# Two-layer hybrid decoder step, one core: four head groups' mixers rearranged (one delta-net pass, four-page attention, fillers in the gated mixer, weight loads on another queue)

## Chip, cores and metric

One Trainium2 chip, one of its cores. The metric is the device time of one execution in microseconds (us), lower is better. A profiled execution also gives a span, from the first to the last instruction of the program. The engines: PE is TensorE (PEld its weight loads), DVE is VectorE, ACT is ScalarE, POOL is GpSimd, SP is SyncE, which here only issues DMAs. [...]

## The reference

544 tokens (a prompt of 512 and 8 samples of 4) pass two layers; everything is f32. In each layer one input projection (1024 to 3592 columns) feeds four head groups that are 256 wide:

```python
u = x @ p['w_in'][l]
(a_in, a_gb, a_gc, b_qkv, b_a, b_b, b_z,
 c_q, c_f, c_i, c_g, d_q, d_k, d_v) = _split(u, SPLITS)
y_a = a_gb * causal_dwconv(a_gc * a_in)                  # A: gated short conv
y_b = rms_norm(gated_delta(q, k, v, beta, g)) * silu(b_z)  # B: gated delta net
y_c = rms_norm(gla(silu(c_q), k_c, c_i, log_f)) * silu(c_g) # C: HGRN2 (gated linear attention)
y_d = rms_norm(diff_attention(d_q, d_k, d_v))            # D: differential attention
x = layer_norm(ALPHA * x + concat(y_a, y_b, y_c, y_d) @ w_o)
x = layer_norm(ALPHA * x + ffn(x))   # layer 0: SwiGLU; layer 1: top-2-of-8 SwiGLU experts
```

B and C are chunked scans that also carry a state; per chunk B solves a unit-triangular system. D attends, for the prompt, within the 512 tokens; for each sample over 16 cached pages of 128 rows, named by a page table, and its own 4 new rows. The outputs are y, the new K and V rows, and the conv and scan states.

## The kernel before, in words

**Order.** The code is written against a tile framework, which lays down each engine's instruction order at build time: a statement earlier in the program has precedence, a later one is pulled into places where the earlier ones are not ready by the framework's own timing model. [...] A tile pool with `bufs=n` hands out n buffers in turn; a new tile waits until the buffer's last user is done.

**Projections.** All large matmuls run at f32r in three passes (high times high, high times low, low times high). `split_w` (L352) loads a 128-column weight tile of 512 KB into `wraw` (three buffers), SP issuing the DMA (L364); ACT (L368), in the expert layer DVE too (L366), makes the high part `wh` and DVE the low part `wl`. `dense` (L380) then issues 48 matmuls for a tile: 8 k-blocks, three passes, two token halves of 256 and 288 columns (in the trace "st", for its PSUM tiles; all matmuls go through the helper `mm`, L290). `win` (L497) does one tile of `w_in`; there are 29 per layer.

**Mixers** (`mixers`, L477, once per layer). PSUM has eight banks: three for projections (`stp`), three `dx` for D, two `mx` for B and C. In program order, at its end (L1261 to L1287):

- `d_in` (L569): 6 tiles for q, k, v of D; K and V go out by POOL's queue.
- `mix_b` (L712): 7 tiles with the conv, gates and norms. Then `g_half` (L811) twice, each for two of the four heads and all four chunks. It builds the 128x128 systems, gathers their 16x16 diagonal blocks through DRAM (`sd`, `bk`), solves them by 15 steps of product and sum on DVE over 64 partitions (L888 is the sum), writes them back through DRAM (`te`), doubles the inverse to 32, 64 and 128 by small matmuls, and runs the four-chunk recurrence. A sample part follows. The second half shares the first half's buffers (`GB = 1`).
- `d_attn` (L588): `d_sample` (L596) has two groups of four samples, and in each 16 steps of one page a sample. A step loads four pages of 256 KB (K and V together, SP's queue, nine buffers that the heads share, L616), takes scores with 8 matmuls (`qs` as weights, 32 columns, each sample in its own column group, 128 keys as moving data), row maximum (L632), exponential with sum (L634), one transpose (L635), a copy on DVE (L637), 4 value matmuls, and on DVE a masked product `r` and its sum (L603) into `pj`. After every second step comes one of 16 prompt `d_head`s (L676), with two score matmuls of 32 rows, one after the other, each into a `dx` bank, and a third bank for the transposed weights. `rms_d` (L536) norms D's and B's output.
- `dc.close()` (L1278), then `hook`, which loads the residual for the next norm into the memory that is freed.
- `mix_a` (L1231): 6 tiles. Then `mix_c` (L1072): 8 tiles; per token half-width `i` seven decay levels over 512 tokens (POOL subtracts, ACT exponentiates, DVE multiplies, `level`, L1106), four chunks of some 45 small matmuls (64x32, 64x64, 32x32), a sample part. Then 2 tiles of `b_z`.
- The four outputs are split into high and low parts and go to `out_proj` (L1445).

Of the kernel before, what the change touches and what calls it, by code (L numbers as in the profile page):

```python
# [10 lines left out]
F32 = mybir.dt.float32  # L11
# [4 lines left out]
OP = mybir.AluOpType  # L16
# [23 lines left out]
KVB = 9  # L40
# [5 lines left out]
ARR = 6  # L46
# [140 lines left out]
def _pack(a):  # L187
# [19 lines left out]
    f["kv"] = _cols(np.concatenate([kp, a["cache_v"].reshape(L, npool, 128, 256)], 3))  # L207
# [58 lines left out]
def _body(ctx, tc, I, O):  # L266
# [15 lines left out]
    stp = pool(ctx, "stp", 3, PSUM)  # L282
# [66 lines left out]
    wq = [S] * WQ0  # L349
    wpools, wcount = [wp], [0]  # L350

    def split_w(parts, n):  # L352
# [10 lines left out]
        for a, src in enumerate(parts):  # L363
            (wq.pop(0) if wq else SP).dma_start(r if na == 1 else r[:, a], src)  # L364
# [112 lines left out]
    def mixers(l, y32, hook):  # L477
# [5 lines left out]
        xps = pool(mc, "mx%d" % l, 2, PSUM)  # L483
# [13 lines left out]
        def win(n, i):  # L497
            w = first.pop(0) if first else load_w(I["w_in"][l, WT0[n] + i])
            res = halves(stp, "st")
            dense(res, w, xh, xl, KT)  # L500
            return res
# [67 lines left out]
        def d_in():  # L569
            q = win_arr("d_q", 32.0 ** -0.5, y32[:, 6:8])  # L570
            k = win_arr("d_k")
            G.dma_start(O["k"][l].rearrange("a p t -> p a t"), k)
            v = win_arr("d_v")
# [14 lines left out]
        def d_attn(q, k, vt, qs):  # L588
            heads = [d_head(q, k, vt, qb, tl, h2) for qb in range(4) for tl in range(2) for h2 in range(2)]
            for n, _ in enumerate(d_sample(k, vt, qs)):  # L590
                if n % 2 == 1:
                    heads[n // 2]()
            for i in range(2):
                rms_d(y32[:, 6:8], i, nd[:, l:l + 1])

        def d_sample(k, vt, qs):  # L596
            od = y32[:, 6:8]
            ends = []

            def select(pj, po):  # L600
# [4 lines left out]
            regs = []  # L605

            def page(i):
                if i == len(regs):
                    with ExitStack() as qx:
                        if len(ends) > 8:  # L610
                            qx.enter_context(tc.issue_after(ends[-9].ins))
                        _, r = nc.values_load_multi_w_load_instructions(ptb[:, i:i + 8], engines=[mybir.EngineType.SP],
                                                                        min_val=0, max_val=I["kv"].shape[1] - 1)
                    regs.extend(r)
                t = dq.tile([128, 512], F32, name="kv", bufs=KVB)
                ends.append(SP.dma_start(t, I["kv"][l][bass.ds(regs[i], 1)].rearrange("o p f -> p (o f)")))  # L616
                return t

            for g in range(2):
                nm = dq.tile([128, 20], F32, name="nm", bufs=2)  # L620
                zz = dq.tile([128, 20], F32, name="zz", bufs=2)
                pj = dq.tile([128, 17, 64], F32, name="pj", bufs=1)
                for j in range(16):
                    kv = [page(64 * g + 4 * j + b) for b in range(4)]
                    ps = dx()
                    for tl in range(2):
                        for b in range(4):
                            mm(ps[32 * b:32 * b + 32, 0:128], qs[:, tl, 4 * g + b, :], kv[b][:, 128 * tl:128 * tl + 128],
                               start=tl == 0, stop=tl == 1)
                    if j == 15:  # L630
                        tt(V, ps[:, 0:128], ps[:, 0:128], bs[:, 0:128], OP.add)
                    V.reduce_max(nm[:, j:j + 1], ps[:, 0:128], axis=AX.X, negate=True)  # L632
                    e = dq.tile([128, 128], F32, name="e", bufs=3)
                    S.activation(e, ps[:, 0:128], AF.Exp, bias=nm[:, j:j + 1], accum_out=zz[:, j:j + 1])  # L634
                    PE.transpose(ps[:, 128:256], e, ident)  # L635
                    et = dq.tile([128, 128], F32, name="et", bufs=3)
                    V.tensor_copy(et, ps[:, 128:256])  # L637
                    for b in range(4):
                        mm(ps[32 * b:32 * b + 32, 256:512], et[:, 32 * b:32 * b + 32], kv[b][:, 256:512])
                    select(pj[:, j], ps[:, 256:512])  # L640
                    yield
# [5 lines left out]
                V.reduce_max(nm[:, 16:17], ps[:, 0:32], axis=AX.X, negate=True)  # L647
                sn = dq.tile([128, 32], F32, name="sn", bufs=1)
                S.activation(sn, ps[:, 0:32], AF.Exp, bias=nm[:, 16:17], accum_out=zz[:, 16:17])
                pe = dx()  # L650
                PE.transpose(pe[0:32, 0:128], sn, ident)
                etn = dq.tile([32, 128], F32, name="etn", bufs=1)
                V.tensor_copy(etn, pe[0:32, 0:128])
                po = dx()
                for b in range(4):
                    mm(po[32 * b:32 * b + 32, 0:256], etn[:, 32 * b:32 * b + 32], vt[0:32, 4, :])
                select(pj[:, 16], po[:, 0:256])
                V.tensor_reduce(nm[:, 17:18], nm[:, 0:17], axis=AX.X, op=OP.min)
                wj = dq.tile([128, 17], F32, name="wj", bufs=1)
                S.activation(wj, nm[:, 0:17], AF.Exp, bias=nm[:, 17:18], scale=-1.0)  # L660
                tt(V, zz[:, 0:17], zz[:, 0:17], wj, OP.mult)
# [1430 lines left out]
```

## Time and profile before

| | us |
|---|---|
| median of 3 runs (2251.12 to 2275.32) | 2256.49 |
| the profiled execution | 2249.46 |
| its span | 2247.8 |
| mixers of layer 0, from the last projection of `mix_b` to the first full out-projection | 108 to 487 |
| mixers of layer 1, the like | 1075 to 1434 |

The profiled execution's 2249.46 us is its span and 1.7 us around it. The page counts as busy what an engine's instructions cover; a matmul's end is modelled, so that TensorE's busy share says little of its pace. Its pace is read from the count of matmuls in a stretch (x) and from the distance between starts.

### The profile page before, as it was taken

What the parts mean: (1) busy time and instruction counts of PE and PEld (TensorE: products, weight loads), DVE (VectorE), ACT (ScalarE), POOL (GpSimd) and SP (SyncE); (2) the same over time, 40 slices, a digit from 0 to 9 for tenths busy, and PEclk for the clock granted to TensorE, in tenths of its full rate; (3) what the DMA queues carried; (4) which work ended last, traced back from release to release, by engine and by line L of the source; (5) the groups of instructions that cost most, each with busy time, mean ns of one, the idle gap of its engine ahead of it and who ended that gap; (6) DMA issues with size and microseconds to landing.
All of it is one profiled execution on the core that took longest, in us unless ns stands there. A gap on an engine that the chain in (4) does not pass through costs nothing.

```text
span 2247.8 us, 47097 instructions
## 1 busy us (share of the span) xinstructions
PE 2094.8 (93%) x18052; PEld 1846.0 (82%) x18052; DVE 1495.4 (67%) x2944; ACT 821.1 (37%) x1842; POOL 460.7 (20%) x588
## 2 busy tenths in 40 slices
PE   8999999998999999999999999888999998898896
PEld 7977776778999999989777667777899897797885
DVE  4676755767333334645767666679989987777795
ACT  3522424455231223444324344434333433433221
POOL 0101012112000000111110221003514436535431
PEclk9999997989999999999999999889999899999998
DMA  6344343233322323542444343337778686586751
GB/s 236 99 125 145 112 144 111 87 118 102 95 79 84 100 86 90 173 160 87 150 126 131 116 131 97 119 113 247 252 235 272 205 278 200 174 264 202 270 190 61
DMA packets 147314, 340.92 MB, mean 152 GB/s; under 512 B 24099, under 2 KB 34568, under 8 KB 147080
## 3 DMA queue, kind: packets, MB, share of 16 engines
q1 hardware_dynamic: 131944, 317.02, 44.0%
q0 software_dynamic: 6032, 18.67, 2.5%
q10 hardware_dynamic: 9104, 2.13, 0.5%
q8 instruction: 144, 2.36, 0.4%
q14 instruction: 90, 0.74, 0.1%
HBM read 319.91 MB, written 17.85 MB: 150 GB/s over the span
## 4 chain that ended last, share of the span: by engine, by line
PE 68%; DVE 12%; POOL 7%; issue 5%; ACT 4%; DMA 4%; DVEq 0%; SPq 0%; ACTq 0%; POOLq 0%
PE st L290 34%; PE ff L290 12%; PE mx L290 9%; PE dx L290 8%; DVE wl L293 3%; POOL m_g L293 2%; PE ee L290 2%; POOL m_u L293 2%; DVE wh L366 2%; ACT wh L368 1%; POOL hg L293 1%; POOL r L1402 1%; ACT ev L1668 1%; DMA sd<-d 1%; DMA wraw<-in_m_g_dram 1%
## 5 line engine op out<-in xcount | busy, mean ns | idle before, releaser
L293 DVE TENSOR_TENSOR wl<-wraw,wh 128x1024 fp32r<-128x1024 f32 (+2 forms) x474 | 562.0, 1194 | 284.8 <-ACT wh L368 261.4
L290 PE MATMUL st<-xh,wh 128*128 128x256 f32 (+1 forms) x1536 | 465.4, 304 | 15.0 <-ACT wh L368 11.6
L290 PE MATMUL st<-xl,wh 128*128 128x256 f32 (+1 forms) x1536 | 462.0, 301 | 8.4 <-DVE xl L293 8.4
L290 PE MATMUL st<-xh,wl 128*128 128x256 f32 (+1 forms) x1536 | 461.4, 301 | 1.8 <-DVE wl L293 1.8
L368 ACT ACTIVATE wh<-wraw 128x1024 fp32r<-128x1024 f32 (+2 forms) x280 | 274.0, 980 | 480.6 <-PE st L290 281.8
L290 PEld LDWEIGHTS st<-xh,wh 128*128 128x128 f32 x1536 | 297.6, 194 | 32.8 <-ACT wh L368 12.7
L290 PEld LDWEIGHTS st<-xl,wh 128*128 128x128 f32 x1536 | 297.8, 194 | 25.7 <-issue 13.4
L290 PEld LDWEIGHTS st<-xh,wl 128*128 128x128 f32 x1536 | 297.3, 194 | 22.0 <-issue 17.7
L290 PE MATMUL st<-xg,wh 128*128 128x416 f32 (+4 forms) x880 | 253.7, 363 | 28.1 <-ACT ev L1668 26.1
L290 PE MATMUL st<-xg,wl 128*128 128x208 f32 (+4 forms) x880 | 217.9, 248 | 4.1 <-DVE wl L293 3.7
L290 PEld LDWEIGHTS st<-xg,wh 128*128 128x128 f32 x880 | 171.1, 194 | 35.8 <-ACT ev L1668 33.1
L290 PEld LDWEIGHTS st<-xg,wl 128*128 128x128 f32 x880 | 173.7, 197 | 9.1 <-DVE wl L293 9.0
L366 DVE CAST wh<-wraw 128x1024 fp32r<-128x1024 f32 (+2 forms) x194 | 158.9, 819 | 21.3 <-PE ee L290 12.0
L290 PE MATMUL st<-hg,wh 128*128 128x416 f32 (+4 forms) x440 | 126.8, 366 | 2.5 <-POOL hg L293 2.2
L1402 POOL TENSOR_SCALAR r<-r,par 128x256 f32<-128x256 f32 (+1 forms) x32 | 29.2, 924 | 467.6 <-ACT xh L1401 467.5
L290 PE MATMUL st<-hg,wl 128*128 128x208 f32 (+4 forms) x440 | 110.2, 251 | 2.1 <-DVE wl L293 2.1
L290 PE MATMUL ff<-hh,wl 128*128 128x256 f32 (+1 forms) x352 | 103.2, 293 | 3.3 <-DVE wl L293 3.2
L290 PE MATMUL st<-wh,xg 128*128 128x256 f32 x528 | 104.7, 292 | 0.0
L290 PE MATMUL ff<-hh,wh 128*128 128x256 f32 (+1 forms) x352 | 103.0, 293 | 0.4 <-ACT wh L368 0.4
L290 PE MATMUL ff<-hl,wh 128*128 128x256 f32 (+1 forms) x352 | 102.1, 290 | 0.0
L290 PE MATMUL ff<-xh,wl 128*128 128x256 f32 (+1 forms) x352 | 101.8, 289 | 0.0
L290 PE MATMUL ff<-xl,wh 128*128 128x256 f32 (+1 forms) x352 | 101.6, 289 | 0.0
(580 smaller groups left out, 4324.5 us busy)
## 6 DMA issues: line engine op xcount, KB each, us to landing
kv<-in_kv_dram SPq DMA_DIRECT2D x256, 256.0 KB, 3.8
wraw<-in_w_in_dram SPq DMA_DIRECT2D x57, 512.0 KB, 3.7
wraw<-in_m_g_dram SPq DMA_DIRECT2D x54, 512.0 KB, 4.3
wraw<-in_m_u_dram SPq DMA_DIRECT2D x54, 512.0 KB, 4.3
wraw<-in_m_g_dram SPq DMA_DIRECT2D x65, 256.0 KB, 4.2
wraw<-in_m_u_dram SPq DMA_DIRECT2D x65, 256.0 KB, 4.6
wraw<-in_w_o_dram SPq DMA_DIRECT2D x32, 512.0 KB, 3.5
wraw<-in_m_d_dram SPq DMA_DIRECT2D x40, 384.0 KB, 3.6
```

The costliest lines, as they stand in the source:

```text
L290: return PE.matmul(out, lhsT, rhs, start=start, stop=stop)
L293: return e.tensor_tensor(out, a, b, op=op)
L366: V.tensor_copy(h, r)
L368: S.activation(h, r, AF.Copy)
L1402: G.tensor_scalar(ri[:, u], ri[:, u], gcol[:, u:u + 1], bcol[:, u:u + 1], op0=OP.mult, op1=OP.add)
L1668: S.activation(t[:, 0:2 * cap], ps[:, 0:2 * cap], AF.Copy)
```

## The change

What it does, part by part:

- **B**: `mix_b` becomes `b_in` (projections), `b_chunks` and `b_sample`. `b_chunks` does all four heads in one pass: 16 systems at once, one gather through DRAM, one substitution over 128 partitions, one recurrence with both token halves in a chunk step. The output overwrites v.
- **D**: K and V pages are two tensors; a step takes four pages of four samples. Scores of 512 keys fill one bank, in 16 matmuls of 256 moving columns (two pages each), now with the sample as the outer loop and the two 128-row parts inside; one maximum, one exponential, four transposes, one copy on ACT, 16 value matmuls that add up in PSUM, one masked product and sum. Seven buffers hold two pages of K or V each. A group has 4 steps, not 16. A head's two score matmuls are issued together, its transposed weights reuse a score bank, and one scaling moves from DVE to ACT. Heads are spread over 20 yields.
- **Order**: `d_in`, `b_in`, `b_chunks`, `c_in` (six tiles of C), `d_attn`, `hook`; then `b_sample` and `mix_c`, whose levels are made per 256 tokens, with four yields. At each yield two fillers run: `mix_a`'s two rows, its stores, z 0, z 1, g 0, g 1 (z with B's norm and gate).
- **Weights**: within the mixers POOL's queue issues the weight loads, not SP's.
- **PSUM**: `dx` 3, `mx` 3, projections 2 within the mixers; the three-bank pool opens behind them.

```diff
-KVB = 9
+KVB = 5
+PGB = 7
-ARR = 6
+ARR = 5
...
-            (wq.pop(0) if wq else SP).dma_start(r if na == 1 else r[:, a], src)
+            (wq.pop(0) if wq else wdef[0]).dma_start(r if na == 1 else r[:, a], src)
...
-        xps = pool(mc, "mx%d" % l, 2, PSUM)
+        xps = pool(mc, "mx%d" % l, 3, PSUM)
+        stm = pool(mc, "st%d" % l, 2, PSUM)
...
             for n, _ in enumerate(d_sample(k, vt, qs)):
-                if n % 2 == 1:
-                    heads[n // 2]()
+                while done < 16 and done < (n + 1) * 16 / 20:
+                    heads[done]()
+                    done += 1
...
-                for j in range(16):
-                    kv = [page(64 * g + 4 * j + b) for b in range(4)]
+                for j in range(4):
+                    regs = indices(64 * g + 16 * j)
                     ps = dx()
-                    for tl in range(2):
-                        for b in range(4):
-                            mm(ps[32 * b:32 * b + 32, 0:128], qs[:, tl, 4 * g + b, :], kv[b][:, 128 * tl:128 * tl + 128],
-                               start=tl == 0, stop=tl == 1)
+                    for u in range(2):
+                        for b, t in enumerate(pages("kc", regs, u)):
+                            for tl in range(2):
+                                mm(ps[32 * b:32 * b + 32, 256 * u:256 * u + 256], qs[:, tl, 4 * g + b, :],
+                                   t[:, :, 128 * tl:128 * tl + 128], start=tl == 0, stop=tl == 1)
...
+                    e = soft(ps, j, 512)
+                    yield
+                    for a in range(4):
+                        PE.transpose(ps[:, 128 * a:128 * a + 128], e[:, 128 * a:128 * a + 128], ident)
+                    et = big("et", 512)
+                    S.activation(et, ps, AF.Copy)
+                    for u in range(2):
+                        vs = pages("vc", regs, u)
+                        for a in range(2):
+                            for b in range(4):
+                                o = 128 * (2 * u + a) + 32 * b
+                                mm(ps[32 * b:32 * b + 32, 0:256], et[:, o:o + 32], vs[b][:, a], start=2 * u + a == 0, stop=2 * u + a == 3)
+                    select(pj[:, j], ps[:, 0:256])
                     yield
...
             for i in range(2):
-                kq = {s: level(s, i, 0, NP_) for s in (64, 32, 16, 8, 4, 2, 1)}
...
                 for c in range(4):
+                    if c % 2 == 0:
+                        kq = {s: level(s, i, c0, 256) for s in (64, 32, 16, 8, 4, 2, 1)}
+                        if c:
+                            yield
...
+        wdef[0] = G
+        bk_, bq_, dk_, ck_, cb_ = [arr() for _ in range(5)]
         dq_, dk_, vt, qs = d_in()
...
+        bk_, bq_, ob, gt_, be, ber, kde, bge, eg_s, kd_s, be_s = b_in()
         with ExitStack() as sc:
-            ob = mix_b(pool(sc, "bp%d" % l))
+            b_chunks(pool(sc, "bp%d" % l), bk_, bq_, ob, gt_, be, ber, kde, bge)
+        kk, cb_, cq_, oc = c_in()
         d_attn(dq_, dk_, vt, qs)
-        for i in range(2):
-            rms_d(ob, i, P("norm_b")[:, l:l + 1])
         dc.close()
         hook()
-        mix_a()
...
         with ExitStack() as sc:
+            sp = pool(sc, "sp%d" % l)
+            cq = pool(sc, "cq%d" % l)
+            b_sample(sp, bk_, bq_, ob, gt_, eg_s, kd_s, be_s)
+            ya = arr()
+            am = mix_a(ya)
+            fills = [lambda: next(am, 0), lambda: next(am, 0), lambda: next(am, 0), lambda: fill_z(0), lambda: fill_z(1),
+                     lambda: fill_g(0), lambda: fill_g(1)]
+            for _ in mix_c(cq, sp, kk, cb_, cq_, oc):
+                for f in fills[0:2]:
+                    f()
+                del fills[0:2]
+            for f in fills:
+                f()
+        wdef[0] = SP
```

## Rows read from the trace of the kernel before

**Rows 1.** The page, section 1: busy us, share of the span, instructions.

```profile
PE 2094.8 (93%) x18052; PEld 1846.0 (82%) x18052; DVE 1495.4 (67%) x2944; ACT 821.1 (37%) x1842; POOL 460.7 (20%) x588
```

**Rows 2.** Stretches: start:end, us, busy us of PE, PEld, DVE, ACT, POOL (instructions); granted clock, DMA share, GB/s.

```profile
108.00:360.00 252.00, 240.31 (x2453) 179.56 (x2452) 172.54 (x497) 85.90 (x225) 33.87 (x59) 0.95 0.43 134
360.00:487.00 127.00, 124.51 (x1452) 85.48 (x1451) 78.60 (x202) 57.59 (x179) 18.24 (x34) 0.85 0.28 85
465.00:487.00 22.00, 20.38 (x116) 12.74 (x114) 12.40 (x27) 10.72 (x27) 1.48 (x3) 0.69 0.31 99
575.00:900.00 325.00, 324.90 (x2580) 324.70 (x2579) 112.30 (x166) 91.30 (x146) 0.00 (x0) 1.00 0.29 88
1075.00:1300.00 225.00, 215.94 (x2243) 163.08 (x2242) 159.16 (x466) 76.33 (x201) 28.09 (x54) 0.96 0.43 134
1300.00:1434.00 134.00, 125.20 (x1610) 86.75 (x1608) 87.92 (x226) 63.51 (x198) 20.11 (x36) 0.94 0.30 91
1410.00:1434.00 24.00, 16.70 (x64) 9.34 (x64) 17.03 (x32) 15.46 (x42) 1.11 (x2) 0.71 0.15 49
```

**Rows 3.** Stretches again, the projections' tile st alone: PE, PEld, DVE, ACT.

```profile
108.00:487.00 379.00, 146.00 (x801) 113.94 (x800) 4.16 (x13) 10.05 (x26) 0.91 0.38 117
1075.00:1434.00 359.00, 134.56 (x766) 105.40 (x764) 3.88 (x12) 9.34 (x24) 0.95 0.38 118
```

**Rows 4.** TensorE in order of time, 342 to 351 us: start, length, what, records.

```profile
342.18 0.62 PE L290 MATMUL dx<-kv,qs 128*32 128x128 f32 x10
342.73 0.39 PE L290 MATMUL st<-xl,wh 128*128 128x256 f32 x1
...
343.07 0.28 PE L290 MATMUL st<-xh,wh 128*128 128x256 f32 x1
343.19 0.28 PE L290 MATMUL st<-xl,wh 128*128 128x256 f32 x1
343.40 0.41 PE L290 MATMUL dx<-kv,qs 128*32 128x128 f32 x2
343.74 0.91 PE L290 MATMUL dx<-arr,y 32*128 32x384 f32 x2
344.57 0.33 PE L635 MATMUL dx<-cst,e 128*128 128x128 f32 x1
...
350.56 0.64 PE L290 MATMUL dx<-kv,et 128*32 128x256 f32 x8
351.13 0.40 PE L290 MATMUL st<-xl,wh 128*128 128x288 f32 x1
```

**Rows 5.** The page loads' DMA issues, layer 0: duration min/median/max ns, first and last start.

```profile
L616 SPq DMA_DIRECT2D kv<-in_kv_dram x128: 332/333/992, 33.0 to 424.1; - x128
```

**Rows 6.** The chain that ended last, layer 1's mixers: start, us, what.

```profile
1412.46 1.90 DVE rd L669
```

**Rows 7.** DVE's groups, 108 to 487 us: count | busy us, mean ns | idle before, releaser.

```profile
L603 DVE TENSOR_REDUCE pj<-r 128x64 f32<-128x256 f32 x32 | 19.0, 595 | 0.1
L293 DVE TENSOR_TENSOR r<-dx,cst 128x256 f32<-128x256 f32 x32 | 13.5, 420 | 16.4 <-PE dx L290 16.1
L637 DVE COPY et<-dx 128x128 f32<-128x128 f32 x30 | 8.5, 287 | 9.0 <-PE dx L635 8.7
L888 DVE TENSOR_REDUCE tb<-tm 64x1 f32<-64x1 f32 (+14 forms) x30 | 6.8, 226 | 0.3
```

**Rows 8.** A DMA issue on POOL, 0 to 487 us, as POOL's groups show it.

```profile
L572 POOL DMA_DIRECT2D out_k_dram<-arr x1 | 0.7, 727 | 38.1 <-ACT arr L507 38.1
```

**Rows 9.** DMA issues: count, KB each, median us to landing.

```profile
wraw<-in_w_in_dram SPq DMA_DIRECT2D x57, 512.0 KB, 3.7
```

**Rows 10.** Waits, 108 to 487 us: who <- for whom: us, times, longest.

```profile
POOL lt L989 <- PE dx L290: 72.3, 1, 72.3
...
POOL diag L293 <- DVE sml L1152: 68.7, 15, 11.5
POOL stga L1248 <- DVE row L293: 57.3, 2, 47.8
```

More of the change, by code (lines that the diff above doesn't have):

```diff
@@ L281, in _body @@
     drp = pool(ctx, "drp", 1, bass.MemoryType.DRAM)
-    stp = pool(ctx, "stp", 3, PSUM)
+    stq = [None]
     xc = ExitStack()
@@ L349, in _body @@
     wq = [S] * WQ0
+    wdef = [SP]
     wpools, wcount = [wp], [0]
@@ L603, in select, with indices @@
                 V.tensor_reduce(pj, r4.rearrange("p h v -> p v h"), axis=AX.X, op=OP.add)
-            regs = []
-            def page(i):
-                if i == len(regs):
+            def indices(i):
+                out = []
+                for o in (0, 8):
                     with ExitStack() as qx:
[L610 to L617, printed above, removed]
@@ new lines, in indices, with pages @@
+                        if len(ends) > PGB:
+                            qx.enter_context(tc.issue_after(ends[-PGB - 1].ins))
+                        _, r = nc.values_load_multi_w_load_instructions(ptb[:, i + o:i + o + 8], engines=[mybir.EngineType.SP],
+                                                                        min_val=0, max_val=I["kc"].shape[1] - 1)
+                    out.extend(r)
+                return out
+            def pages(src, regs, u):
+                out = []
+                for b in range(4):
+                    t = dq.tile([128, 2, 256], F32, name="pg", bufs=PGB)
+                    for a in range(2):
+                        ends.append(SP.dma_start(t[:, a], I[src][l][bass.ds(regs[4 * (2 * u + a) + b], 1)].rearrange("o p f -> p (o f)")))
+                    out.append(t)
+                return out
@@ new lines, in hs, with b_chunks, wk @@
+        def hs(h):
+            return slice(64 * (h % 2), 64 * (h % 2) + 64)
+        def b_chunks(bp, k, q, v, gt_, be, beh, kde, bge):
+            def wk(w=512):
+                return bp.tile([128, 512], F32, name="wk", bufs=3)[:, 0:w]
+            lt = bp.tile([128, 16, 128], F32, name="lt", bufs=1)
+            pt = bp.tile([128, 16, 128], F32, name="pt", bufs=1)
+            kt = bp.tile([128, 2, 4, 128], F32, name="kt", bufs=1)
+            erl = bp.tile([128, 2, 4], F32, name="erl", bufs=1)
+            for i in range(2):
+                hh = slice(2 * i, 2 * i + 2)
@@ new lines, in b_chunks, with w16, t32 @@
+                    S.activation(er, ep[:, 0:256], AF.Exp)
+                    V.tensor_copy(erl[:, i, cc], er.rearrange("p (c t) -> p c t", c=2)[:, :, 127])
+                    tt(V, q[:, i, t2], q[:, i, t2], er, OP.mult)
+            def w16(ap):
+                return ap.rearrange("p (a b) -> p a b", a=16)
+            def t32():
+                return w16(bp.tile([128, 512], F32, name="t32", bufs=3))
+            me, mo = C("me"), C("mo")
+            lc = t32()
+            for u in range(4):
+                sl = slice(32 * u, 32 * u + 32)
+                S.activation(lc[sl], lt[sl, :, sl], AF.Copy)
@@ new lines, in b_chunks @@
+            tt(V, T_, T_, w16(tq), OP.subtract)
+            tt(V, TT, TT, w16(tr), OP.subtract)
+            for u in range(4):
+                sl = slice(32 * u, 32 * u + 32)
+                S.activation(lt[sl, :, sl], TT[sl], AF.Copy)
+            t64 = bp.tile([128, 1056], F32, name="inv", bufs=1)[:, 0:1024].rearrange("p (a b) -> p a b", a=16)
+            xq = mx()
+            x = w16(wk())
+            for u in range(2):
+                ra, rb = slice(64 * u, 64 * u + 32), slice(64 * u + 32, 64 * u + 64)
+                for a in range(16):
+                    mm(xq[rb, 32 * a:32 * a + 32], lt[ra, a, rb], T_[ra, a])
+                tt(V, x[rb], w16(xq)[rb], bc(beh[rb], 32), OP.mult)
@@ L1179, in mix_c @@
                     G.dma_start(O["hp"][l, hs(h), i], st[hs(h), 64 * h:64 * h + 64])
+                yield
             sm = slice(NP_, T)
-            s0 = [bp.tile([128, NB, 64], F32, name="kq512", bufs=7) for _ in range(2)]
+            s0 = [sp.tile([128, NB, 64], F32, name="s2k", bufs=3) for _ in range(2)]
             for i in range(2):
@@ L2029, in _body @@
         r = held[-1]
-        for i, (c0, nn) in enumerate(HALVES):
-            for k in range(KT):
-                hilo(xh[i][:, k], xl[i][:, k], y32[:, k, c0:c0 + nn])
         if l == 0:
             with ExitStack() as fc:
+                stq[0] = pool(fc, "stp", 3, PSUM)
                 fp = pool(fc, "fp")
```

450 lines of the change are left out of this document (220 added, 230 removed).

## Prediction

> **What bounds the kernel now.** I read the page's first section, then the span cut into stages, then TensorE's instructions in order of time, and last the waits. TensorE is busy 93% of the span [rows 1], so the question is what its busy time is worth. In the dense feed-forward of layer 0 (575 to 900 us) it issues 2580 matmuls in 325 us, one per 0.126 us: that is full pace. The two mixer stages are slower: 108 to 487 us in layer 0, 1075 to 1434 in layer 1 [rows 2]. There 801 and 766 of the matmuls are projection work ("st") [rows 3]; at full pace they need 801 x 0.126 = 101 and 97 us. The other 278 and 262 us are small f32 matmuls, the price of breaking off and resuming, and lost clock.
>
> [Rows 4] price the breaks. Projection matmuls start 0.12 us apart. A foreign piece starts 0.21 after the last of them, so 0.09 is lost ahead of it, and a piece of one 128-column f32 matmul (two records) lasts 0.34, while ten records last 0.55. Ten records are a first matmul and four that run beside each other in the four column groups, so each further round of 128 columns costs 0.21, and the fixed part of a piece is 0.34 - 0.21 = 0.13. A piece thus costs 0.09 + 0.13 + 0.21 per round. The eight-record piece of 256 columns, 0.57, and the single 384-column matmul, 0.83 = 0.13 + 3 x 0.21 and a little, fit.
>
> Three more things stand in the rows. The granted clock is 0.95 and 0.85 in layer 0's two stages, 0.96 and 0.94 in layer 1's [rows 2], 0.91 and 0.95 over the whole stretches [rows 3]: (1 - 0.91) x 379 = 34 us and (1 - 0.95) x 359 = 18 us are the most that it takes. The page loads of the attention go on until 424 us in layer 0 [rows 5], and in layer 1 its last sum starts at 1412.5 [rows 6]: the 32 page steps of a layer end with the mixers, not before. And so both stages end in a tail (465 to 487, 1410 to 1434) with 116 and 64 matmuls, at a clock of 0.69 and 0.71 [rows 2]. TensorE in the mixers is what I price; DVE is 68% busy there (172.5 of 252), and its waits count where TensorE idles: 252 - 240.3 = 12 and 225 - 215.9 = 9 us.
>
> **The change part by part**, per layer.
>
> *Pages in fours.* Scores before, as the rows show the pattern: three pieces of one matmul as the pages come (0.43 each) and one of ten records (0.55 + 0.09), 32 steps: 32 x 1.93 = 62 us. After, 16 groups of four page pairs, each pair two matmuls of 256 columns in one column group (four rounds): 0.09 + 0.13 + 4 x 0.21 = 1.06. One pair at a time it is 64 x 1.06 = 68 us; four in one piece, where a pair's second matmul runs beside the next pair's first, ten rounds: 16 x 2.32 = 37. I take 60, since single pieces are the pattern now: -2, bounds -25 and +6. Values: before 32 x (0.57 + 0.09) = 21. After, in one piece of four rounds 16 x 1.06 = 17; with three pairs apart (0.64 each, then 1.06) 16 x 2.98 = 48. They arrive while the softmax runs, so I take 20: -1, bounds -4 and +27. Transposes in fours save 24 breaks of about 0.1: -2. Sum -5 (-31 to +31).
>
> DVE loses 24 of 32 of the masked product (0.42) and of its sum (0.59), and the copies (0.29 x 32) go to ACT [rows 7]: 24 x 1.01 + 9 = 33 us. The substitution's 15 steps run once on 128 partitions, not twice on 64: 15 reductions of 0.23 less [rows 7]. One DRAM round trip pair goes as well. None of it is TensorE's; it shortens waits. I take half of the idle: -6 and -5 (bounds 0, -12 and -9).
>
> *Heads.* The two score matmuls of a head now come together, on different 32 rows, with three PSUM banks where the head needed all three. A second matmul beside the first saves 0.21 x (1 to 4), 0.53 in the mean, and a break of 0.22: 16 x 0.75 = 12 us; 0 if the banks come singly. I take -6.
>
> *Attention that ends earlier.* 8 steps in place of 32, each with one softmax chain, release the tail: two of the three norm stages behind it (the attention's and, as a filler, the delta-net's) move ahead. Of tails of 22 and 24 us I take -10 each (0 to -15).
>
> *Fillers.* The 6 a-projections, 2 z and 2 g come between the quarters of the HGRN scan in place of ahead of or behind it; before, that stretch had little projection work and the clock fell there to 0.85. Work only moves: eight more tiles there, eight fewer beside the attention, cut into pieces in both. The clock gets back half: -17 and -9 (bounds 0, and -34 and -18). If each moved tile is cut into six more pieces than now, 8 x 6 x 0.22 = 11 us come back; if into six fewer, as much goes.
>
> [...]
>
> *One delta-net pass.* The matmuls stay; fewer, longer pieces are in the heads' terms' noise, and I cost them at nothing (0 to -5). The single chain is hidden by the attention; without that cover it would be one half's stretch, and no longer than now.
>
> *POOL fetches, two banks.* 56 weight loads move past SP's page loads into POOL's queue, where a DMA issue is 0.73 us [rows 8]: 20 us a layer on an engine busy 52 of 379 us. 512 KB land in 3.7 us from SP [rows 9]. TensorE takes 48 x 0.126 = 6 us a tile and three raw buffers are 18 us of lead, so I cost it at nothing but the layer's first loads among POOL's norm work. A third PSUM bank less for the projections leaves one half, 3 us, for ACT's copy. Together +3 (0 to the rival below).
>
> *Sum.* Layer 0: -5 - 6 - 6 - 10 - 17 + 3 = -41. Layer 1: -5 - 5 - 6 - 10 - 9 + 3 = -32. Together -73 on the profiled execution's 2249.5: 2176.5. The median of the three runs is 7.0 above that execution; the changed kernel's should stand alike: **2183 us**. One per cent, 22.6 us, is about what can be told from no change.
>
> **Rivals.** *The attention was the whole trouble (deeper).* If the 32-step chain sets the order of all else, then clock (-34, -18), heads (-12 each), tails (-15 each) and idle (-12, -9) go whole: with -5 and +3 a layer that is -131, 2125. For it: attention and mixers end together in both layers. Against: TensorE idles only 12 us.
>
> *Pairs one at a time (no change).* Scores at 68 and values at 48 cost +31 in place of -5: 72 us more in two layers, -1, 2255. For it: single pieces are what the rows show for keys. Against: values wait for the softmax anyway.
>
> *The page ring keeps the attention long.* Seven pair buffers hold less than half of a step's 16 pairs. If the loads then pace it to the end, tails and clock stay: -73 + 20 + 26 = -27, 2229. Against: DMA engines are 0.43 busy.
>
> *POOL's queue starves TensorE (slower).* POOL stood 72.3 us behind one wait and 47.8 behind another in this stretch, 68.7 in 15 waits at one line [rows 10]. A weight load behind such a wait comes late, and TensorE's queue is in order, so all behind the first projection matmul waits too. The lead is 18 - 3.7 = 14 us; the two long waits would expose 58 + 34 = 92 us a layer: -73 + 184 = +111, 2367. It decides from 37 us exposed a layer. Against: the order is fixed at build time with these waits in view.
>
> [...]
>
> **How the numbers follow.** Forecast 0.50 (2150 to 2215), deeper 0.17, ring 0.10, pairs 0.13, POOL 0.10. The range reaches down over most of the deeper case and up over the pairs: 2115 to 2262. Faster by over 1% (under 2234): 0.50 + 0.17 and most of the ring, 0.75. Within 1%: pairs and the rest of the ring, 0.14. Slower: POOL and a pairs case that loses the tails too, 0.11.
>
> **What would show it.** Right: layer 0's last page load well before 424 us; the granted clock from 360 us on above 0.93; fewer than 32 DVE sums per layer at the masked product; out-projections starting some 40 and 70 us earlier. Wrong: score pieces of four records that make its group longer than now; TensorE waiting for a weight conversion whose load came late from POOL; a tail as thin as now. If the mixers shrink but the clock there does not rise, the fillers' term is wrong.

## The result and the profile after

The changed kernel takes 2277.05 us (median of 20 runs, 2266.89 to 2292.28), the kernel before 2253.6 us beside it (20 runs): a ratio of 1.011, 95% interval 1.0085 to 1.0135. It is slower by 23 us, where 2183 us were forecast; 2277 lies above the range too. The profiled execution took 2278.61 us, with a span of 2276.8. The first full out-projection of layer 0 ends 14 us later than before (502.6 for 488.5, start of its first evacuation on DVE) and that of layer 1 34 us later (1472.6 for 1438.4); the expert layer gives 5 us back.

The page of the changed kernel, section 1, answers to [rows 1]:

```profile
PE 2115.4 (93%) x17620; PEld 1849.2 (81%) x17620; DVE 1389.3 (61%) x2632; ACT 825.1 (36%) x1782; POOL 495.8 (22%) x694
```

DVE has lost 106 us of work, as meant. TensorE has 432 matmuls fewer and is busy 21 us longer. The mixers, cut as in [rows 2] (same columns), with the tails of both layers and the thinnest stretch of layer 0:

```profile
108.00:503.00 395.00, 377.14 (x3724) 274.00 (x3724) 207.22 (x555) 146.23 (x375) 61.91 (x138) 0.90 0.39 112
284.00:328.00 44.00, 41.00 (x295) 23.34 (x294) 19.83 (x55) 9.97 (x27) 8.59 (x18) 0.63 0.42 124
328.00:430.00 102.00, 100.27 (x845) 63.89 (x845) 51.20 (x142) 36.82 (x105) 24.96 (x59) 0.96 0.44 129
430.00:481.00 51.00, 50.59 (x721) 42.95 (x721) 33.94 (x86) 33.46 (x97) 4.55 (x10) 1.00 0.24 77
481.00:503.00 22.00, 20.89 (x179) 17.08 (x179) 11.65 (x24) 10.27 (x20) 1.11 (x2) 0.77 0.16 49
1075.00:1472.00 397.00, 382.21 (x3830) 280.98 (x3829) 212.67 (x582) 155.64 (x394) 63.16 (x144) 0.94 0.39 116
1446.00:1472.00 26.00, 24.60 (x210) 20.65 (x209) 15.29 (x37) 13.02 (x28) 2.95 (x6) 0.80 0.14 44
```

And of these the projections' tile st alone, as in [rows 3]:

```profile
108.00:503.00 395.00, 137.16 (x862) 117.84 (x863) 4.63 (x15) 10.46 (x27) 0.90 0.39 112
284.00:328.00 44.00, 0.74 (x6) 0.50 (x5) 0.82 (x2) 0.00 (x0) 0.63 0.42 124
```

The two clocks of [rows 3], 0.91 and 0.95, are now 0.90 and 0.94 (where the dense feed-forward of [rows 2] has 1.00): nothing came back. From 328 to 481 us, where the scan and its fillers stand, it is 0.96 and 1.00; from 284 to 328 us, with 6 projection matmuls, it is 0.63. The page loads' DMA issues in layer 0, as in [rows 5], for keys and values:

```profile
L633 SPq DMA_DIRECT2D pg<-in_kc_dram x128: 332/333/1925, 33.2 to 405.8; - x128
L633 SPq DMA_DIRECT2D pg<-in_vc_dram x128: 332/333/1277, 82.5 to 425.3; - x128
```

The attention's last page load comes as late as before (424.1); its last sum on DVE (`rd`) starts 9 us earlier, at 442.8 for 451.7 us. Its scores and values on TensorE, from the groups of instructions, both layers (count | busy us, mean ns | idle before, releaser); first the kernel before:

```profile
L290 PE MATMUL dx<-kv,qs 128*32 128x128 f32 x1024 | 94.7, 294 | 0.3 <-DMA kv<-in_kv_dram 0.3
L290 PE MATMUL dx<-kv,et 128*32 128x256 f32 x512 | 44.7, 402 | 0.5 <-DVE et L637 0.5
```

then the changed kernel:

```profile
L292 PE MATMUL dx<-pg,qs 128*32 128x256 f32 x512 | 102.8, 387 | 1.5 <-DVE y L701 0.8 <-DMA pg<-in_kc_dram 0.7
L292 PE MATMUL dx<-pg,kv 128*32 128x256 f32 x512 | 65.3, 426 | 0.0
```

Together 139.4 us before, 168.1 after: 28.7 us more, against a loss of 23. This was the first suspect. TensorE of the changed kernel in order of time, 79 to 89 us, shows why:

```profile
80.48 0.29 PE L292 MATMUL st<-xh,wl 128*128 128x288 f32 x1
80.70 1.08 PE L292 MATMUL dx<-pg,qs 128*32 128x256 f32 x16
81.72 1.18 PE L292 MATMUL mx<-row,cst 128*128 128x256 f32 x4
...
83.83 0.49 PE L292 MATMUL dx<-arr,y 32*128 32x128 f32 x4
84.47 1.02 PE L292 MATMUL dx<-pg,qs 128*32 128x256 f32 x4 [0.15 <-DMA pg<-in_kc_dram]
```

A piece of four samples (16 records) lasts 1.08 us, a piece of one sample (4 records) 1.02. The four column groups run beside each other, so three more samples cost 0.06 us when they come together, and a whole piece each when they come apart. Counted over layer 0, scores are 49 pieces, 36 of them of one sample, and values 36 pieces, 15 of them one matmul, mostly of 0.55 us.

### The profile page after: what moved, and what is told of

The parts are those of the page before. It is cut to its first block, busy times and chain, and to the rows that moved or that the text cites. A ratio compares the mean times of both kernels' runs of the same rounds, so it can differ in the third digit from the quotient of the medians.

```text
span 2276.8 us, 46714 instructions
## 1 busy us (share of the span) xinstructions
PE 2115.4 (93%) x17620; PEld 1849.2 (81%) x17620; DVE 1389.3 (61%) x2632; ACT 825.1 (36%) x1782; POOL 495.8 (22%) x694
## 5 line engine op out<-in xcount | busy, mean ns | idle before, releaser
L292 PE MATMUL st<-xg,wh 128*128 128x416 f32 (+4 forms) x880 | 248.2, 357 | 31.3 <-ACT ev L1739 28.6
L367 POOL DMA_DIRECT2D wraw<-in_w_in_dram x56 | 30.8, 550 | 350.2 <-DVE wl L295 266.1
L292 PE MATMUL dx<-pg,qs 128*32 128x256 f32 x512 | 102.8, 387 | 1.5 <-DVE y L701 0.8
```

Of the source, the lines that this page charges most:

```text
L292: return PE.matmul(out, lhsT, rhs, start=start, stop=stop)
L367: (wq.pop(0) if wq else wdef[0]).dma_start(r if na == 1 else r[:, a], src)
```

## The experiments

Three theories. **S**: TensorE pays for scores and values in pieces of one sample. **F**: the attention and the delta net stand in a lump with too little projection work beside them, so waits and a low granted clock (0.63 from 284 to 328 us) cost more. **P**: the weights come late through POOL's queue. Every ratio is to the kernel before, run beside it on the same chip; "busy" is the sum of the two groups above (139.4 before, 168.1 after). On these chips the kernel before took 2245 to 2259 us (medians), so the ratios compare and the medians do not. By the intervals, two ratios have to lie 0.004 to 0.008 apart to be told from each other.

| run | ratio | 95% interval | median us | busy us |
|---|---|---|---|---|
| changed kernel | 1.011 | 1.0085 to 1.0135 | 2277.05 | 168.1 |
| e1 scores turned | 1.0049 | 1.0019 to 1.008 | 2261.23 | 142.6 |
| e2 SP fetches | 1.013 | 1.0089 to 1.0172 | 2277.14 | 158.9 |
| e3 old attention | 1.0563 | 1.0527 to 1.0599 | 2377.63 | 153.0 |
| e4 new attention alone | 1.0054 | 1.0019 to 1.009 | 2264.17 | 164.2 |
| e5 last first | 0.9865 | 0.9804 to 0.9925 | 2233.19 | 85.9 |
| e6 HGRN tiles behind | 1.0123 | 1.0066 to 1.0181 | 2291.81 | 172.4 |
| e7 sample part early | 1.0009 | 0.9973 to 1.0046 | 2263.72 | 163.9 |
| e8 e4, last first | 0.9868 | 0.9817 to 0.9919 | 2235.92 | 88.4 |
| e9 values last first | 1.0043 | 1.0009 to 1.0078 | 2252.63 | 141.3 |
| e10 before, last first | 0.9999 | 0.9966 to 1.0032 | 2246.45 | 90.2 |
| e11 e5 and e7 | 0.9817 | 0.9767 to 0.9867 | 2203.82 | 84.8 |
| e12 fillers outside | 1.0184 | 1.0131 to 1.0236 | 2287.6 | 169.8 |
| e13 heads apart | 1.0139 | 1.009 to 1.0188 | 2278.86 | 167.6 |
| e14 e11, three banks | 0.9699 | 0.965 to 0.9748 | 2179.8 | 79.7 |
| e15 three banks alone | 1.012 | 1.0078 to 1.0162 | 2281.87 | 174.3 |
| e16 e5, three banks | 0.9828 | 0.9795 to 0.9862 | 2202.66 | 83.6 |
| e17 e7, three banks | 1.0108 | 1.0083 to 1.0132 | 2272.02 | 172.5 |

### What the parts are worth: e1 to e4

**e1**, the changed kernel with the two score loops exchanged:

```diff
-                        for b, t in enumerate(pages("kc", regs, u)):
-                            for tl in range(2):
+                        ks4 = pages("kc", regs, u)
+                        for tl in range(2):
+                            for b, t in enumerate(ks4):
```

> The changed kernel with the score loops turned: all four page pairs of a group are loaded, then the two 128-row parts are the outer loop and the four samples the inner one, as before the change. Theory S (scores and values in series on TensorE are the loss): a pair's two matmuls no longer wait for each other in one column group; the scores' share of TensorE falls from some 52 us a layer to 30 to 40, and the time from 2277 to 2240 to 2255. Theory F (attention stands in a lump without projection work beside it, so that waits and the low clock are the loss): 2265 to 2277. Theory P (POOL's queue delivers weights late): 2277.

0.6% back, half of the loss: 2261 us lies between the ranges of S and F. Busy time fell by 25.5 us.

**e2**, the weights on SP's queue again:

```diff
-        wdef[0] = G
+        wdef[0] = SP
```

> The changed kernel with the mixers' weight loads back on SP's queue. Theory P: POOL's late loads are the loss, so 2240 to 2260. Theories S and F: no difference that can be told, 2270 to 2285; SP's queue then carries page and weight loads, which may hold weights up a little.

1.013: no difference from 1.011. P falls. In the changed kernel POOL's weight issues are short:

```profile
L367 POOL DMA_DIRECT2D wraw<-in_w_in_dram x56 | 30.8, 550 | 350.2 <-DVE wl L295 266.1 <-DVE ax L754 22.3 <-DVE wk L918 16.5
```

**e3**, the changed kernel with the attention of the kernel before (`d_sample`, `d_head`, `d_attn` and the joint tensor of K and V as they were):

```diff
-KVB = 5
-PGB = 7
+KVB = 9
...
-                for j in range(4):
-                    regs = indices(64 * g + 16 * j)
+                for j in range(16):
+                    kv = [page(64 * g + 4 * j + b) for b in range(4)]
```

> The changed kernel with the attention of before (one page a step, keys and values in one 256 KB load, nine buffers), all else as changed. Theory S: the attention's 22 us a layer on TensorE come back and the rest of the change is worth something: 2215 to 2240. Theory F: the lump stays, so 2265 to 2285. If it is over 2290, the new attention is a gain and the rest of the change the loss.

**e4**, the reverse: the kernel before with the new attention and nothing else (the same lines the other way round, in the kernel before).

> The kernel before with the changed attention alone (four pages a step, pages in pairs, heads spread over 20 yields). Theory S: 22 us a layer more on TensorE, less some waits: 2270 to 2295. Theory F: a gain or nothing, 2225 to 2255, since projections still lie beside the attention.

With the old attention the rest of the change loses 127 us (1.0563), far above the ranges of both theories: by the last sentence put ahead of e3, the new attention is a gain beside the rest of the change. With the new attention the rest loses 0.6% (1.011 for 1.0054). e4 lies between the ranges of S and F. The page loads of layer 0 differ, first e3:

```profile
L618 SPq DMA_DIRECT2D kv<-in_kv_dram x128: 332/333/2107, 34.1 to 501.8; - x128
```

then e4:

```profile
L631 SPq DMA_DIRECT2D pg<-in_kc_dram x128: 332/333/1266, 33.9 to 336.8; - x128
L631 SPq DMA_DIRECT2D pg<-in_vc_dram x128: 332/333/1708, 86.4 to 354.0; - x128
```

The order in which the rest of the change lays the work holds a 32-step chain of pages until 501.8 us. The 8-step chain alone, in the old order, ends at 354, 70 us before that of the kernel before, and yet e4 is not faster. It has the same seven page buffers as the changed kernel, so it is not these alone that hold the loads there until 425 us. Its stage still ends in a tail, in the columns of [rows 2]:

```profile
470.00:492.00 22.00, 18.31 (x137) 13.98 (x131) 9.07 (x20) 5.82 (x13) 2.21 (x4) 0.63 0.07 26
```

So an attention that ends 70 us earlier does not take the tail away. But e4 also pays for its pieces (164.2 us busy for 139.4); e8 takes that away.

### The pieces: e5, e8, e9, e10

**e5**, the changed kernel with the loops of e1 and, in scores and values, the sample whose pages are loaded last taken first. Its first matmul then waits for all four (ahead of the scores TensorE stood 9.5 us behind K pages, for 0.7 in the changed kernel, both layers), and the others stand right behind it, in pieces of 16 or 8 records:

```diff
+                        ks4 = pages("kc", regs, u)
+                        for tl in range(2):
+                            for b in (3, 2, 1, 0):
+                                t = ks4[b]
...
-                            for b in range(4):
+                            for b in (3, 2, 1, 0):
                                 o = 128 * (2 * u + a) + 32 * b
```

> The changed kernel with the score loops turned (part outside, sample inside) and, in scores and values, the sample whose pages come last taken first, so that a piece's matmuls stand behind one wait and run together. Theory S (TensorE pays for pieces of scores and values that run in series): score time per layer from about 45 to about 34 us and value time from 29 to about 17 us, so 2235 to 2250 us (the turned loops alone gave 2261). Rival F (the stage is set by too little projection work beside the attention and the sample part, whatever the pieces cost): no better than the turned loops alone, 2256 to 2266.

**e8**, the same two edits on e4.

> The kernel before with the new attention (alone 2264), with the loops turned and the last pages first as in e5. Theory S: 2 x 20 us less than with the new attention as it is, so 2222 to 2242 us, faster than the kernel before (2254). Rival: the pieces' cost is made up elsewhere, 2255 to 2266.

**e9**, the changed kernel with the second edit alone (values).

> The changed kernel with only the value matmuls turned to last pages first; the scores stay in the changed kernel's order. Theory S: the values' time falls from 29 to about 19 us per layer as in e5, two layers make 20 us, so 2253 to 2266 us, some 40 per cent of the gain of e5. If only the scores matter, 2272 to 2284.

All three went the way that S says: 2.5% off the changed kernel, 1.9% off e4, 0.7% for the values alone (each give or take 0.4 to 0.7). e8 lies in its range, e5 is 2 us below it; the values alone are 27 per cent of e5's gain, not 40. The two groups in e5:

```profile
L292 PE MATMUL dx<-pg,qs 128*32 128x256 f32 x512 | 45.4, 419 | 11.1 <-DMA pg<-in_kc_dram 9.5 <-issue 1.4
L292 PE MATMUL dx<-pg,kv 128*32 128x256 f32 x512 | 40.5, 431 | 10.4 <-DMA pg<-in_vc_dram 9.5 <-ACT kv L665 0.7
```

Busy time falls by 82 us and 20 us of waiting for pages come instead (the idle column): 62 us net, against 55 measured (2.45% of 2254; the profiled spans differ by 45). In order of time the pieces of e5 (225 to 250 us) are whole, or cut once with all four samples in each half (8 records); in layer 0 scores come in 21 pieces for 49, values in 18 for 36:

```profile
225.70 1.07 PE L292 MATMUL dx<-pg,kv 128*32 128x256 f32 x16
...
233.95 1.07 PE L292 MATMUL dx<-pg,qs 128*32 128x256 f32 x16
...
241.78 0.64 PE L292 MATMUL dx<-pg,qs 128*32 128x256 f32 x8
```

**e10**, the same idea in the kernel before, one page a sample and step, was to say whether the number of pages matters at all:

```diff
                     for tl in range(2):
-                        for b in range(4):
+                        for b in (3, 2, 1, 0):
...
-                    for b in range(4):
+                    for b in (3, 2, 1, 0):
                         mm(ps[32 * b:32 * b + 32, 256:512], et[:, 32 * b:32 * b + 32], kv[b][:, 256:512])
```

> The kernel before, attention with one page a sample and step as it was, but the sample whose page comes last taken first in scores and values. Theory S says that the number of pages in a step is not what matters, but the pieces: 32 steps of one score piece of 16 records (0.09 + 0.55 or so) in place of 62 pieces, scores 41 to about 22 us a layer, so 2210 to 2230 us. Rival: with nine page buffers for two steps of four, the scores now wait for the last page of each step and TensorE stands, 2245 to 2275.

A miss for S as it was put. The scores did come in fewer pieces (38 and 39 for 95 and 91), busy time fell by 49 us, and the time did not move (0.9999). The page loads of e10 still end at 424.5. Layer 0's mixers, their end and the whole, are this (in the columns of [rows 2], then TensorE in order of time):

```profile
465.00:492.00 27.00, 17.50 (x60) 11.31 (x61) 14.05 (x31) 14.89 (x37) 0.00 (x0) 0.56 0.22 69
108.00:491.00 383.00, 349.19 (x3922) 269.20 (x3921) 250.69 (x703) 145.33 (x405) 51.28 (x93) 0.85 0.37 114
```

```profile
466.29 0.43 PE L290 MATMUL dx<-cst,rd 128*64 128x32 f32 x4 [2.88 <-DVE rd L670]
466.65 1.22 PE L290 MATMUL dx<-kv,cst 128*128 128x256 f32 x2
468.77 1.33 PE L290 MATMUL dx<-kv,cst 128*128 128x288 f32 x2 [0.90 <-ACT kv L540]
470.99 1.22 PE L290 MATMUL dx<-kv,cst 128*128 128x256 f32 x2 [0.90 <-ACT kv L540]
```

The last attention sum (`rd`) is there at 466 us, 12 us later than in the kernel before (454), and eight norm steps follow in series, one every 2.2 us, until 483. So in e10 the 32-step chain ends the stage; in the kernel before its norm steps run from 455 to 477 us, beside the scan's last matmuls. What the pieces saved went into waiting and into the clock: from 108 us on TensorE is idle for 34 us (383 - 349.2), where it was 14, and the granted clock is 0.85, where it was 0.91 [rows 3]. Which of the two brought the other about no run shows. The two halves of the four-page attention need each other: the short chain with its broken pieces gives 1.0054, whole pieces alone 0.9999, both 0.9868.

### Theory F: e6, e7, e11

**e6**, the changed kernel with `c_in` and `d_attn` exchanged:

```diff
-        kk, cb_, cq_, oc = c_in()
         d_attn(dq_, dk_, vt, qs)
+        kk, cb_, cq_, oc = c_in()
```

> The changed kernel with the six projection tiles of the HGRN mixer put behind the attention in program order, so that they are there to fill in beside it. Theory F: 30 us of projection work move from before 176 us into the thin stretch 200 to 330 us, its granted clock of 0.6 to 0.9 rises, 2255 to 2268 us. Theory S: the pieces stay as they are, 2272 to 2282 us.

1.0123, no better than 1.011. The attention ends 47 us earlier (last page load at 377.9 us), and the thin stretch now has 59 projection matmuls for 6 and a clock of 0.95 for 0.63:

```profile
284.00:328.00 44.00, 43.81 (x270) 23.88 (x269) 26.59 (x85) 12.67 (x34) 13.86 (x33) 0.95 0.44 127
```

What theory F asked for came about there, and nothing is gained. That the six tiles are used up early costs nothing that can be told.

**e7**, the delta net's sample part right behind its chunks:

```diff
             b_chunks(pool(sc, "bp%d" % l), bk_, bq_, ob, gt_, be, ber, kde, bge)
+        with ExitStack() as sc:
+            b_sample(pool(sc, "bs%d" % l), bk_, bq_, ob, gt_, eg_s, kd_s, be_s)
...
-            b_sample(sp, bk_, bq_, ob, gt_, eg_s, kd_s, be_s)
             ya = arr()
```

> The changed kernel with the delta net's sample part moved from behind the attention to right behind its chunks, where its chain of small matmuls no longer holds up the short convolution's output buffer, the z tiles and the two projection banks. Theory B (the fillers are blocked until the sample part is done at 305 us): projection matmuls appear between 284 and 328 us, where there are 6 now, 2255 to 2268 us. If that stretch costs nothing, 2272 to 2282; if the chain now holds up the attention instead, over 2282.

**e11**, the edits of e5 and e7 together.

> The changed kernel with both mends: last pages first in scores and values with turned loops (e5: ratio 0.9865), and the delta net's sample part right behind its chunks (e7: ratio 1.0009 where the changed kernel has 1.011). If the two causes are separate, the gains add: ratio 0.973 to 0.980, 2195 to 2214 us. If the thin stretch from 284 to 328 us is the same loss that the pieces cause, 0.984 to 0.989, 2220 to 2234.

e7 gives 1.0%, e11 0.5% over e5, give or take 0.8, which may be nothing; the gains add to less than forecast (0.9817, just outside 0.973 to 0.980). The stretch from 284 to 328 us has changed as expected, here e11, all and st alone:

```profile
284.00:328.00 44.00, 42.53 (x516) 30.82 (x519) 35.66 (x114) 25.02 (x83) 23.42 (x56) 0.99 0.46 133
```

```profile
284.00:328.00 44.00, 16.97 (x96) 13.30 (x95) 0.98 (x3) 0.79 (x2) 0.99 0.46 133
```

96 projection matmuls for 6, and a clock of 0.99 for 0.63. But the reason I gave is not shown: in e7 the sample part's 64 state matmuls run only 12 us sooner (285.3 for 297.6 us). What else changed in the order laid around it, and which of it gave the 1.0%, is open.

### Fillers, heads, banks: e12 to e17

**e12**, the changed kernel with the fillers out of the HGRN scan:

```diff
+            for f in fills[0:3]:
+                f()
             for _ in mix_c(cq, sp, kk, cb_, cq_, oc):
-                for f in fills[0:2]:
-                    f()
-                del fills[0:2]
-            for f in fills:
+                pass
+            for f in fills[3:]:
                 f()
```

> The changed kernel (ratio 1.011) with the fillers out of the HGRN scan in program order: the three pieces of the short convolution ahead of it, z and g tiles behind it, as in the kernel before. The prediction's fillers' term says the stage loses 17 + 9 us of clock: 2295 to 2310 us. If the framework pulls the tiles into the same places wherever they are written, 2268 to 2286. If cutting them into pieces costs more than the clock gives, below 2265.

1.0184: 0.7% slower (17 us, give or take 13 by the two intervals). 2287.6 us lies just above the second range; the ratio alone would put it at 2295, the edge of the first. The fillers in the scan do help, by about two thirds of the 26 us forecast. But it does not show as clock; e12's mixers in the columns of [rows 2]:

```profile
108.00:505.00 397.00, 378.88 (x3771) 274.72 (x3770) 209.31 (x563) 147.84 (x378) 60.36 (x139) 0.93 0.39 114
1075.00:1480.00 405.00, 385.79 (x3788) 280.98 (x3786) 210.19 (x576) 153.16 (x389) 60.67 (x141) 0.91 0.37 112
```

Counted as in the prediction, the clock takes at most (1 - 0.93) x 397 = 28 and (1 - 0.91) x 405 = 36 us without the fillers, and 40 and 24 with them: 64 us both times.

**e13**, a head's two score matmuls apart again, one loop doing both:

```diff
                     pss.append(ps)
-                for m, ps in enumerate(pss):
                     tt(V, ps[:, b0:nk], ps[:, b0:nk], bt[:, h, 256 - (nk - b0):256], OP.add)
```

> The changed kernel with a head's two score matmuls again issued one by one, each followed by its own maximum and exponential. The prediction's heads' term (6 us a layer, up to 12) says 2285 to 2305 us. If the banks come singly or the matmuls run beside each other anyway, 2270 to 2284.

1.0139 for 1.011, 6.5 us, give or take 12: the forecast 12 us fit, and so does nothing at all.

**e14**, e11 with PSUM shared as before in the mixers:

```diff
-        xps = pool(mc, "mx%d" % l, 3, PSUM)
-        stm = pool(mc, "st%d" % l, 2, PSUM)
+        xps = pool(mc, "mx%d" % l, 2, PSUM)
+        stm = pool(mc, "st%d" % l, 3, PSUM)
```

> The version with both mends (e11, ratio 0.9817) with PSUM shared as before, three banks for projections and two for the small matmuls of the two scans. The prediction's term of +3 us a layer for the bank less says 5 us faster, 2195 to 2203 us; if the third bank for the scans is worth more, 2208 to 2225.

**e15**, the same edit on the changed kernel alone; **e16** on e5; **e17** on e7.

> The changed kernel (ratio 1.011) with nothing but PSUM shared as before: three banks for projections and two for the scans' small matmuls. If the gain of e14 over e11 (0.9817 to 0.9699, 1.2 per cent) is the bank itself, the same 1.2 per cent here: ratio 0.995 to 1.003, 2240 to 2258 us. The prediction's size for it, 3 us a layer, says 1.008, 2268 to 2275. If the bank helps only where the pieces have been mended, 1.011 or more.

> The changed kernel with the pieces mended (as e5, ratio 0.9865) and three banks for projections, the sample part where it was. If the bank pays once the pieces are whole (their number no longer grows with the projections in between, as it did in e15: score pieces 45 to 50 in layer 0), 0.974 to 0.982, 2198 to 2218 us. If it pays only once the sample part is out of the way, 0.984 to 0.990.

> The changed kernel with the sample part early (as e7, ratio 1.0009) and three banks for projections, the pieces as they were. If the bank pays once the sample part is out of the way, 0.985 to 0.993, 2222 to 2242 us. If it pays only with whole pieces, 0.998 to 1.004, 2248 to 2266; if both runs show nothing, the step from e11 to e14 needs both mends or lies in how the order happened to be laid.

| ratio | two banks | three banks |
|---|---|---|
| changed kernel | 1.011 | 1.012 |
| sample part early | 1.0009 | 1.0108 |
| whole pieces | 0.9865 | 0.9828 |
| both | 0.9817 | 0.9699 |

e14 is faster than both of its ranges, e15 fits the last of its three cases, e16 falls between its two, and e17 is slower than all of its cases. Whole pieces give 1.9 to 4.1% in all four pairs: the one effect that is shown whatever stands beside it. The early sample part gives 0.1 to 1.3%, the bank between 1.0% lost and 1.2% won, each give or take 0.4 to 0.8. The bank wins for certain only in e14. Each of these edits also lays the whole order anew, and how much of the smaller differences is that, no run shows. On the changed kernel the bank does not pay; the score pieces go from 49 and 48 to 53 and 49, and their busy time in e15 rises from 102.8 to 112.2 us, which is more than five pieces of 1 us:

```profile
L292 PE MATMUL dx<-pg,qs 128*32 128x256 f32 x512 | 112.2, 425 | 1.1 <-DMA pg<-in_kc_dram 0.8 <-DVE y L701 0.3
```

e14, at 0.9699 and 2179.8 us, beats both kernels by 3 and 4%.

## Why the prediction was wrong, step by step

The profiled span rose by 29.0 us (2276.8 for 2247.8) where 73 less were forecast: 102 us to explain. The terms below miss by 37 us (pieces), 20 (tails), 38 (clock), 12 (DVE's waits), up to 12 (heads) and -6 (fetches and banks), 113 in all. The clock of the tails stands in two of them, so this is an account and not a measured split.

**"Pages in fours", the step that failed.** "I take 60, since single pieces are the pattern now: -2", and values "arrive while the softmax runs, so I take 20: -1". The single pieces came, at 0.98 to 1.02 us as priced (1.06 with the 0.09 ahead). Two things were mis-sized. The scores before were priced at 62 us a layer by a pattern of 32 equal steps; taken from all starts in order of time with 0.09 ahead of each piece they are 51 and 48 (42.7 us of 95 pieces, 39.9 of 91), so that 54 and 53 after (49 and 48 pieces) are a loss of 3 and 5. And the values are 37 and 31 us, not 20, against 24 and 21 before: they come apart by page just as the keys do, and with the last page first they come whole (e9: 20 and 18 pieces for 36 and 33). Sum +16 and +15 for -3 and -3, 37 of the 102 us; it was inside the bounds of -31 to +31. The rival "pairs one at a time" had the mechanism, with 68 us for the scores and 48 for the values too dear, and I gave it 0.13. Also wrong was the pricing of a full piece: "ten rounds: 16 x 2.32". Four samples together take 1.08 us, hardly more than one, and whole pieces came to 27 and 21 us a layer in e5 (25.2 us of 21 pieces, 18.9 of 20, with 0.09 each), below the low bound of 37. With this step mended and nothing else (e5) the time falls by 55 us: more than the loss of 23, and half of the 102.

**"Attention that ends earlier", -10 a layer.** The last page load did not come earlier (425.3 for 424.1), and the last sum only by 9 us. In e4 the short chain alone does end 70 us earlier (with 25 us more of pieces), in e6 47 us, with no gain. The rival of the page ring foresaw loads that last to the end, but e4 and e6, with the same seven buffers, end early. The tails are 22 and 26 us long as before; they hold more work (179 and 210 matmuls for 116 and 64 in [rows 2]), and their clock is 0.77 and 0.80 for 0.69 and 0.71.

**"Fillers", clock -17 and -9.** The clock in the scan did go from 0.85 [rows 2] to 0.96 and 1.00, and e12 without the fillers loses 17 us. That the number is near is luck as far as the runs go: the clock takes the same 64 us in e12, so the fillers' gain is not shown to be clock. The lost clock of the whole, as counted there, is (1 - 0.90) x 395 = 40 and (1 - 0.94) x 397 = 24 us, 6 more each than the 34 and 18 of before. Work "only moves", the prediction said; it moved out of the stretch ahead of the scan, where the delta net's sample part and the attention now stand almost without projections (0.63, at most (1 - 0.63) x 44 = 16 us; in e6 that stretch is at 0.95 and nothing is gained). What failed here was to count the clock where the tiles go and not where they are taken from. "I cost them at nothing", of the one delta-net pass, was not tried alone.

**DVE's waits, -6 and -5.** DVE did lose the work: 44 us in layer 0 (207.2 for 251.1 busy). TensorE's idle time stayed, 18 and 15 us for 14 and 18 (stretch less busy time): nothing of DVE's 44 us shows in it.

**Heads, -6 each**: unclear (e13). Two score matmuls in one piece do run beside each other: in the changed kernel two of 384 columns took 0.97 us (361.26), one alone 0.91 (340.71). **POOL**: nothing, as the forecast said, and the starvation rival is out: with the fetch on SP the ratio is 1.013 for 1.011 (e2). **Two banks, +3 with POOL**: nothing on the changed kernel (e15), but 1.2% (27 us) in e14 over e11; a term that has no size of its own here, since it changes with what stands beside it.

**The bound.** "TensorE is busy 93% of the span, so the question is what its busy time is worth" was half of it. e10 takes 49 us of these two groups from TensorE and gains nothing; e4 shortens the chain by 70 us, with 25 us more in the groups, and gains nothing; both together gain 1.3% (e8). That fits a kernel that stands on both bounds at once, with the rival "deeper" (the 32-step chain sets the order) as the other half. It is argued and not shown: in e10 the clock fell too, and no run holds it while the chain stays.

The remainder of the 102 us that no run isolates (the single pass, the new order of the parts) is small once the pieces are whole: e5 (0.9865, the whole change) and e8 (0.9868, the attention alone) are equal, within 0.8% or 18 us.

## What to carry to other kernels

When small matmuls of several column groups feed one accumulator, let the first one issued be the one whose data lands last; here the others then ran beside it, and a piece of four samples took 1.07 us (e5, 225.70), where one sample alone took 1.02 (changed kernel, 84.47). Where shortening a chain and relieving an engine each measure as nothing, try both together before giving one up: here they gave 1.3% as a pair. A bank more was worth between -1.0 and +1.2% here, by what stood beside it; in a kernel whose order is laid by a scheduler, measure such a count again after every other mend.

## What the runs showed of the hardware

- The length of a score piece hardly depended on the number of column groups in it: in the changed kernel 1.02 us with one group (84.47), 1.08 with four (80.70).
- What stood behind a waiting matmul in TensorE's queue waited with it: in e5, with the sample loaded last issued first, the scores of the samples loaded earlier did not run ahead. They come in 21 pieces for 49 in layer 0, and TensorE's idle time ahead of them is 11.1 us for 1.5 (both layers).
- A busy TensorE had a low granted clock in one run and a high one in another. In e5, 284 to 328 us, granted 0.50, TensorE is busy 43.2 of 44 us with 391 small matmuls and no projection; in e6 the same stretch is busy 43.8 us with 270 matmuls, 59 of them projections, at 0.95:

```profile
284.00:328.00 44.00, 43.23 (x391) 26.25 (x393) 20.38 (x65) 11.46 (x44) 7.60 (x16) 0.50 0.33 97
```

- The faster kernel had the lower mean clock: e5's mean is 0.933 for 0.949 of the changed kernel, at 45 us less.
- A weight load's DMA issue on POOL took 0.55 us, less than the 0.73 of [rows 8].
